# Bisection of a top-k selection: the decision steps move from VectorE to GpSimd

## The chip, the cores and the metric

The kernel runs on one core of a Trainium2 chip. The metric is the device time of one execution in microseconds (us). The engines are TensorE (PE in the profile, PEld for its weight loads), VectorE (DVE), ScalarE (ACT), GpSimd (POOL) and SyncE (SP). Each engine takes its instructions strictly in the order in which they were written into its queue, and engines wait for each other through semaphores.

## The reference

One layer of an encoder on 2048 tokens of width 1024: a combined projection, a sparse attention in which every query keeps its 256 best keys by an index score, a pooling mixer, gates, an output projection with layer norm, and a gated MLP with a short convolution. The part that the change touches is the choice of the keys:

```
rel = relu(einsum('bqhd,bsd->bqhs', qib, k_idx) * idx_scale)
idx_score = einsum('bqh,bqhs->bqs', wib * head_w_scale, rel)
idx_score = where(admissible, idx_score, -inf)
_, sel = top_k(idx_score, topk)        # topk = 256
...
s = where(valid, einsum('bqhd,bqkd->bqhk', qb, k_sel) * attn_scale, -inf)
p = softmax(s)
```

## The kernel before

The 2048 queries are 16 blocks of 128 rows; a row of a block is one partition. The keys of a block are a mask that is computed ahead of the attention, by finding for each row the 256th largest score.

**Bisection.** `select` (L896) finds that threshold bit by bit: 32 rounds from bit 31 down to bit 0. It works on two *halves* of the blocks in turn, so that the decision on one half can run while the other half is counted. For a half and a bit, every block of the half is counted at the trial threshold `F`: ScalarE counts the back part of the scores with a Sign activation that sums (`ca`, L945), VectorE the front part with a comparison that sums (`cd`, L948). Then `decide` (L917) makes the next threshold from the two sums in three steps on VectorE: `g = 2*cd - ca`, `h = (g < lim) * 2^bit`, `F = h xor 2^(bit-1) xor F`. A decision of one half is a generator (`pend`), and one of its steps is taken after each block of the other half's counting (L950), the rest at that half's end (L953). The tiles of a decision have one number per block, so they are 128x2 or 128x4.

**Three selections.** `GROUPS` (L64) gives three selections: blocks 2 and 3 against 4 to 7 (halves of two and four blocks), then 8 and 9 against 10 and 11, then 12 and 13 against 14 and 15. They run as background work: `turn` (L356) gives them a step whenever the projections on TensorE have earned a credit in a cost model, so index scores, counts and decisions are written between the matmuls of `proj_index`, `proj_pool`, `proj_q` and `proj_gates`, and between the instructions on ScalarE and VectorE that empty PSUM for them. `PS1` (L299) has four PSUM banks for these matmuls.

**GpSimd beside it.** In the first of four token groups the projection weights are split into a rounded part and a remainder (`Weights.split` L237, `split` L309): on GpSimd, in pieces of 256 columns (`PIECE`, L95), a TENSOR_SCALAR for the rounded part and a TENSOR_TENSOR for the remainder. A weight item is two tensors of 128x4x256, so eight pieces; its split is written when the item ahead of it is fetched (`get`, L247). Later token groups reload the parts from DRAM. GpSimd also sums the windows of the pooling mixer (L707). So its queue holds much work in the time of the first selection, and little in the others.

Nearly all compute instructions carry the line of the helper that records them (L150); tiles tell them apart. `b` is a tile of the big pool (scores, weights and their parts), `m` one of the pool of eight middle tiles, `p` a PSUM bank.

Of the kernel before, what the change touches and what calls it, by code (L numbers as in the profile page):

```python
# [15 lines left out]
OP = mybir.AluOpType  # L16
# [3 lines left out]
P = 128  # L20
# [236 lines left out]
class Kern:  # L257
# [638 lines left out]
    def select(self, halves):  # L896
# [6 lines left out]
        nc = self.nc  # L903
# [12 lines left out]

        def decide(k, bit):  # L917
            cd, ca = acc[k]
            nh = len(halves[k])
            g_ = self.sml([P, 4], tag="g")[:, :nh]  # L920
            h = self.sml([P, 4], I32, tag="h")[:, :nh]
            f2 = self.sml([P, 4], I32, tag="F")[:, :nh]
            lim = 2.0 * TOPK - 1.0 - ws[k]
            nc.vector.scalar_tensor_tensor(g_, cd, 2.0, ca, op0=OP.mult, op1=OP.subtract)
            yield
            if bit == 31:
                nc.vector.tensor_scalar(h, g_, lim, -1.0, op0=OP.is_lt, op1=OP.mult)
                yield
                nc.vector.tensor_scalar(f2, h, 0x40000000, None, op0=OP.bitwise_xor)
            else:  # L930
                nc.vector.tensor_scalar(h, g_, lim, float(2 ** bit), op0=OP.is_lt, op1=OP.mult)
                yield
                nc.vector.scalar_tensor_tensor(f2, h, 2 ** (bit - 1) if bit else 0, F[k],
                                               op0=OP.bitwise_xor, op1=OP.bitwise_xor)
            F[k] = f2

        pend = None
        for bit in range(31, -1, -1):
            for k, half in enumerate(halves):
                f = F[k].bitcast(F32)  # L940
                w, nh = ws[k], len(half)
                cd, ca = self.sml([P, 4], tag="cd")[:, :nh], self.sml([P, 4], tag="ca")[:, :nh]
                for i, b in enumerate(half):
                    ja, jd = self.M([P, 1024], BF16), self.M([P, 1024], BF16)
                    nc.scalar.activation(ja[:, :w], back[b], AF.Sign, bias=f[:, i:i + 1], scale=-1.0,  # L945
                                         accum_out=ca[:, i:i + 1])
                    n = front[b].shape[1]
                    nc.vector.tensor_scalar(jd[:, :n], front[b], f[:, i:i + 1], None, op0=OP.is_ge, op1=OP.add,  # L948
                                            accum_out=cd[:, i:i + 1])
                    if pend:  # L950
                        next(pend, None)
                    yield
                if pend:  # L953
                    for _ in pend:
                        pass
                acc[k] = (cd, ca)
                pend = decide(k, bit)
        for _ in pend:
            pass
        for k, half in enumerate(halves):  # L960
            f = F[k].bitcast(F32)
            w, nh = ws[k], len(half)
# [19 lines left out]
            for i, b in enumerate(half):  # L982
# [9 lines left out]
                                               op0=OP.mult, op1=OP.subtract)  # L992
# [882 lines left out]
```

## Time and profile before

| | |
|---|---|
| median of 3 runs | 3335.93 us (3323.9, 3339.29, 3335.93) |
| the profiled execution, own time | 3325.95 us |
| its span, first to last instruction | 3324.2 us |
| PE busy | 3168.4 us (95%), 15918 matmuls |
| DVE busy | 2423.5 us (73%) |
| ACT busy | 1585.2 us (48%) |
| POOL busy | 1271.3 us (38%) |
| mean granted clock of TensorE | 0.981 |

The first selection counts from 210 to 416 us of the span, the second from about 530 to 712 us, the third from about 874 to 1083 us. The rest of the 3324 us is attention, output projection and MLP, which the change doesn't touch. How to read it: a share of the whole span says little here, since 95% for PE is a mean over stages; what counts is which engine waits in the three selections.

### The profile page before, as it was taken

Reading aid. Unit: us, or ns where it says so; the run is one execution under the profiler, and the core shown is the slowest. Engines: PE = TensorE matmul, PEld = TensorE weight load, DVE = VectorE, ACT = ScalarE, POOL = GpSimd, SP = SyncE. Lnnn points to the kernel's source line nnn. Section 1 sums busy time; section 2 is a strip of 40 time slices with the busy share of each in tenths; the row PEclk is TensorE's granted clock in tenths of the full one; section 3 lists DMA queues with packets and bytes.
Section 4 is the critical chain, followed back from the end, with each engine's and each line's share of the span. In section 5 each row is a group of like instructions: output and inputs, shape, how many; then the busy total and the mean of one; then the engine's idle time right before and its main releaser. Section 6 shows DMA issues by size and latency. Waiting matters only on the chain. (4 is left out here: it accounts for less than half of the span.)

```text
span 3324.2 us, 46905 instructions
## 1 busy us (share of the span) xinstructions
PE 3168.4 (95%) x15918; PEld 2658.2 (80%) x15918; DVE 2423.5 (73%) x4475; ACT 1585.2 (48%) x2854; POOL 1271.3 (38%) x1302
## 2 busy tenths in 40 slices
PE   8998899999999899999999989999989999999898
PEld 8887688888898778888878877777868778888687
DVE  5589878996899887777676576666578765555597
ACT  3465737855678566666621133333244432223343
POOL 3139400010010787667731154550066511211684
PEclk9999899999999999999999999999999999999999
DMA  8457755754566344443464458997697665666884
GB/s 323 146 197 279 246 210 186 249 198 145 189 249 224 120 162 173 143 158 145 149 231 161 157 209 319 348 328 278 226 356 273 206 250 221 235 248 244 314 308 167
DMA packets 325679, 745.71 MB, mean 224 GB/s; under 512 B 30074, under 2 KB 115006, under 8 KB 325438
## 3 DMA queue, kind: packets, MB, share of 16 engines
q1 hardware_dynamic: 315646, 724.88, 60.8%
q10 hardware_dynamic: 9792, 17.83, 1.4%
q8 instruction: 126, 2.06, 0.3%
q14 instruction: 115, 0.94, 0.1%
HBM read 514.36 MB, written 228.23 MB: 223 GB/s over the span
## 5 line engine op out<-in xcount | busy, mean ns | idle before, releaser
L150 PE MATMUL p<-b,b 128*128 128x512 f32 (+3 forms) x12644 | 2785.6, 369 | 79.5 <-ACT b L150 20.6
L150 PEld LDWEIGHTS p<-b,b 128*128 128x128 f32 x12644 | 2173.6, 191 | 484.0 <-ACT b L150 23.1
L150 ACT ACTIVATE b<-p 128x512 fp32r<-128x512 f32 (+9 forms) x726 | 428.7, 612 | 667.9 <-PE p L150 628.1
L150 ACT ACTIVATE b<-b 128x1024 fp32r<-128x1024 f32 (+2 forms) x248 | 253.2, 1027 | 397.7 <-POOL b L150 148.9
L150 DVE TENSOR_TENSOR b<-b,b 128x1024 fp32r<-128x1024 f32 (+5 forms) x246 | 358.6, 1488 | 78.9 <-ACT b L150 75.9
L150 ACT ACTIVATE m<-b,F 128x448 bf16<-128x448 f32 (+3 forms) x448 | 366.1, 820 | 84.2 <-DVE F L150 67.3
L150 DVE TENSOR_SCALAR_CACHE_REDUCE m<-b,F 128x512 bf16<-128x512 f32 (+6 forms) x476 | 370.8, 808 | 17.8 <-DMA q<-m 12.4
L150 POOL TENSOR_TENSOR b<-b,b 128x256 fp32r<-128x256 f32 (+3 forms) x276 | 315.9, 1161 | 72.3 <-ACT b L150 66.2
L150 DVE TENSOR_TENSOR m<-m,p 128x512 f32<-128x512 f32 x176 | 120.5, 685 | 245.2 <-ACT b L150 207.0
L150 POOL TENSOR_TENSOR b<-b,m 128x512 f32<-128x512 f32 x110 | 196.7, 1808 | 237.9 <-DMA b<-h 165.3
L150 POOL TENSOR_TENSOR m<-b,b 128x512 f32<-128x512 f32 x99 | 144.4, 1466 | 349.4 <-issue 258.4
L150 DVE SCALAR_TENSOR_TENSOR b<-b,cw,b 128x1023 f32<-128x1023 f32 (+1 forms) x176 | 243.4, 1385 | 35.7 <-ACT b L150 34.5
L150 POOL TENSOR_SCALAR b<-b 128x256 fp32r<-128x256 f32 (+3 forms) x216 | 117.3, 558 | 379.4 <-DMA b<-in_w_in_dram 127.7
L150 PE MATMUL p<-b 128*128 128x512 f32 x616 | 235.8, 399 | 13.2 <-ACT b L150 8.7
L150 DVE TENSOR_TENSOR b<-p,b 128x512 fp32r<-128x512 f32 (+1 forms) x286 | 201.5, 713 | 59.5 <-ACT b L150 57.2
L150 PE MATMUL p<-ident,b 128*128 128x128 f32 x1456 | 214.8, 277 | 20.9 <-ACT b L150 14.4
L150 DVE CUSTOM_DVE_ANT_0 b<-p,b 128x1024 f32<-128x1024 f32 (+7 forms) x192 | 173.9, 908 | 67.4 <-PE p L150 66.1
L150 PEld LDWEIGHTS p<-ident,b 128*128 128x128 f32 x1456 | 176.6, 142 | 53.5 <-ACT b L150 17.5
L150 ACT ACTIVATE b<-b,mx 128x1024 f32<-128x1024 f32 (+7 forms) x192 | 171.6, 896 | 67.2 <-DVE mx L150 63.0
L150 DVE SCALAR_TENSOR_TENSOR b<-b,ws,b 128x768 f32<-128x768 f32 (+5 forms) x154 | 157.4, 1050 | 43.1 <-ACT b L150 41.0
L150 ACT ACTIVATE m<-p 128x512 f32<-128x512 f32 (+1 forms) x180 | 105.4, 593 | 152.9 <-PE p L150 136.9
L150 PE MATMUL p<-kst,b 128*128 128x384 f32 (+3 forms) x656 | 151.6, 361 | 4.5 <-DVE b L150 3.3
(126 smaller groups left out, 2386.7 us busy)
## 6 DMA issues: line engine op xcount, KB each, us to landing
b<-uw SPq DMA_DIRECT2D x308, 512.0 KB, 6.8
b<-wp SPq DMA_DIRECT2D x192, 512.0 KB, 6.2
uw<-l SPq DMA_DIRECT2D x98, 512.0 KB, 2.9
b<-in_w_ffn_down_dram SPq DMA_DIRECT2D x154, 256.0 KB, 5.4
b<-h SPq DMA_DIRECT2D x154, 256.0 KB, 5.4
wp<-b SPq DMA_DIRECT2D x64, 512.0 KB, 5.6
uw<-b SPq DMA_DIRECT2D x56, 512.0 KB, 5.4
h<-m SPq DMA_DIRECT2D x110, 256.0 KB, 5.6
```

The source lines that it names most:

```text
L150: return f(*args, **kw)
```

## The change

`decide` keeps its arithmetic and gets one step more. The two sums are now combined on GpSimd in place, in `cd`: `cd = 2*cd - lim`, then `cd = cd - ca`. The comparison `h = (cd < 0) * 2^bit` follows on GpSimd too. Only the xor stays on VectorE. So a decision was three instructions on VectorE and is three on GpSimd and one on VectorE; there are 192 decisions (three selections, 32 bits, two halves).

```diff
         def decide(k, bit):
             cd, ca = acc[k]
+            pool = nc.gpsimd
             nh = len(halves[k])
-            g_ = self.sml([P, 4], tag="g")[:, :nh]
...
             lim = 2.0 * TOPK - 1.0 - ws[k]
-            nc.vector.scalar_tensor_tensor(g_, cd, 2.0, ca, op0=OP.mult, op1=OP.subtract)
+            pool.tensor_scalar(cd, cd, 2.0, -lim, op0=OP.mult, op1=OP.add)
+            yield
+            pool.tensor_tensor(cd, cd, ca, op=OP.subtract)
             yield
             if bit == 31:
-                nc.vector.tensor_scalar(h, g_, lim, -1.0, op0=OP.is_lt, op1=OP.mult)
+                pool.tensor_scalar(h, cd, 0.0, -1.0, op0=OP.is_lt, op1=OP.mult)
                 yield
                 nc.vector.tensor_scalar(f2, h, 0x40000000, None, op0=OP.bitwise_xor)
             else:
-                nc.vector.tensor_scalar(h, g_, lim, float(2 ** bit), op0=OP.is_lt, op1=OP.mult)
+                pool.tensor_scalar(h, cd, 0.0, float(2 ** bit), op0=OP.is_lt, op1=OP.mult)
                 yield
                 nc.vector.scalar_tensor_tensor(f2, h, 2 ** (bit - 1) if bit else 0, F[k],
                                                op0=OP.bitwise_xor, op1=OP.bitwise_xor)
```

Where the new instructions stand shows in the queues of the built programs. First GpSimd, early in the first selection, at the second weight item that is split there (`b_3030`, `b_3040` the rounded parts of its two tensors, `b_3031`, `b_3041` the remainders; `halo` is the pooling mixer's). Before the change:

```order
L150 COPY b_3020<-halo_93 128x16
L150 COPY b_3023<-halo_93 128x16
L150 TENSOR_SCALAR b_3030<-b_2859 128x256 x2
L150 TENSOR_TENSOR b_3031<-b_2859,b_3030 128x256 x2
L150 TENSOR_SCALAR b_3030<-b_2859 128x256 x2
L150 TENSOR_TENSOR b_3031<-b_2859,b_3030 128x256 x2
L150 TENSOR_SCALAR b_3040<-b_2861 128x256 x2
L150 TENSOR_TENSOR b_3041<-b_2861,b_3040 128x256 x2
L150 TENSOR_SCALAR b_3040<-b_2861 128x256 x2
L150 TENSOR_TENSOR b_3041<-b_2861,b_3040 128x256 x2
```

GpSimd at the same place after the change, from the third decision of the selection (`cd_2968`, `h_2990`) to the first instruction of the fourth (`cd_2984`):

```order
L150 TENSOR_SCALAR cd_2968<-cd_2968 128x2
L150 TENSOR_TENSOR cd_2968<-cd_2968,ca_2969 128x2
L150 TENSOR_SCALAR h_2990<-cd_2968 128x2
L150 TENSOR_SCALAR b_3030<-b_2858 128x256 x2
L150 TENSOR_TENSOR b_3031<-b_2858,b_3030 128x256 x2
L150 TENSOR_SCALAR b_3030<-b_2858 128x256 x2
L150 TENSOR_TENSOR b_3031<-b_2858,b_3030 128x256 x2
L150 TENSOR_SCALAR b_3040<-b_2860 128x256 x2
L150 TENSOR_TENSOR b_3041<-b_2860,b_3040 128x256 x2
L150 TENSOR_SCALAR b_3040<-b_2860 128x256 x2
L150 TENSOR_TENSOR b_3041<-b_2860,b_3040 128x256 x2
L150 TENSOR_SCALAR cd_2984<-cd_2984 128x4
```

The split item itself has not moved; two decisions now stand around it, and the fourth has all of its eight pieces ahead of it. The other decisions of the first selection are placed in the same manner, some ahead of an item, some behind it, some between its pieces.

Then VectorE at the same place. Before the change, the end of the second decision and the third (`g_2974` to `F_2976`, `g_2990` to `F_2992`) among the counts (`m,cd<-b,F`):

```order
L150 TENSOR_SCALAR m_2971,cd_2968<-b_1707,F_2751 128x128
L150 SCALAR_TENSOR_TENSOR g_2974<-cd_2743,ca_2744 128x4
L150 TENSOR_SCALAR h_2975<-g_2974 128x4
L150 TENSOR_SCALAR m_2979,cd_2968<-b_1811,F_2751 128x256
L150 TENSOR_SCALAR F_2976<-h_2975 128x4
L150 TENSOR_SCALAR m_2987,cd_2984<-b_2119,F_2976 128x192
L150 SCALAR_TENSOR_TENSOR g_2990<-cd_2968,ca_2969 128x2
L150 TENSOR_SCALAR h_2991<-g_2990 128x2
L150 SCALAR_TENSOR_TENSOR F_2992<-h_2991,F_2751 128x2
```

VectorE after the change, from the same count on:

```order
L150 TENSOR_SCALAR m_2971,cd_2968<-b_1707,F_2750 128x128
L150 TENSOR_SCALAR F_2975<-h_2974 128x4
L150 TENSOR_SCALAR m_2978,cd_2968<-b_1811,F_2750 128x256
L150 TENSOR_SCALAR m_2987,cd_2984<-b_2119,F_2975 128x192
L150 SCALAR_TENSOR_TENSOR F_2991<-h_2990,F_2750 128x2
```

Two of three instructions of a decision are gone; the xor that is left stands where it stood and reads `h` from GpSimd. The places of ScalarE's counts among its other instructions are the same as before in the first selection, within two instructions, and those of TensorE's matmuls among each other nearly so.

## The prediction

> **What bounds the kernel now.** I read the page's slices first, to see where TensorE falls short.
>
> ```profile
> PE   8998899999999899999999989999989999999898
> DVE  5589878996899887777676576666578765555597
> POOL 3139400010010787667731154550066511211684
> PEclk9999899999999999999999999999999999999999
> ```
>
> A slice is 83 us. TensorE is the limit nearly everywhere; one of its dips, and the one dip of the granted clock below 0.9, lies in slices 3 to 5 (166 to 416 us), where VectorE is at 8 to 9 tenths and GpSimd reaches 9. That is the first selection. The windows view puts numbers on the three selections (the first in two parts):
>
> ```profile
> core 0: us, PE busy (x) PEld busy (x) DVE busy (x) ACT busy (x) POOL busy (x), PEclk, DMA share, GB/s
> ...
> 210.00:335.00 125.00, 105.77 (x626) 94.58 (x624) 115.39 (x314) 74.82 (x226) 106.69 (x194) 0.93 0.77 276
> 335.00:415.00 80.00, 66.25 (x273) 53.16 (x274) 71.40 (x285) 65.01 (x199) 38.70 (x73) 0.87 0.73 253
> ...
> 530.00:712.00 182.00, 176.94 (x905) 151.74 (x904) 163.59 (x507) 144.54 (x314) 6.43 (x15) 0.99 0.68 240
> ...
> 874.00:1083.00 209.00, 207.08 (x1110) 179.37 (x1109) 193.50 (x505) 167.92 (x313) 16.65 (x27) 1.00 0.66 235
> ```
>
> From 530 to 712 and from 874 to 1083 us TensorE is busy 97 and 99% at full clock: there it is the bound, and relief of VectorE is worth at most the 5.1 and 1.9 us that it idles. In the first selection it idles 19.2 + 13.8 = 33 us, and VectorE (92% and 89%) and GpSimd (85% in the first part) are full. The waits view of 210 to 415 us names the chain:
>
> ```profile
> ACT m L150 <- DVE F L150: 43.6, 22, 7.4
> ...
> POOL b L150 <- PE p L150: 18.4, 1, 18.4
> PE p L150 <- ACT m L150: 18.3, 5, 5.4
> ...
> PE p L150 <- ACT b L150: 14.0, 7, 4.8
> POOL b L150 <- DMA b<-in_w_in_dram: 11.2, 2, 10.8
> ```
>
> ScalarE waits 43.6 us for the next threshold `F`, and TensorE 32.3 us for ScalarE, which stands behind its counts. So this stage is set by how fast decisions follow each other.
>
> **Why decisions are slow there.** The groups of `g` and `h` in 210 to 335 us, and from the timeline one `g` with what GpSimd did beside it:
>
> ```profile
> L150 DVE SCALAR_TENSOR_TENSOR g<-cd,ca 128x2 f32<-128x2 f32 x15 | 16.5, 1098 | 4.3 <-ACT m L150 4.2
> ...
> L150 DVE SCALAR_TENSOR_TENSOR g<-cd,ca 128x4 f32<-128x4 f32 x16 | 13.3, 828 | 0.9 <-ACT m L150 0.6
> ...
> L150 DVE TENSOR_SCALAR h<-g 128x2 int32<-128x2 f32 x15 | 7.4, 492 | 0.4
> ...
> L150 DVE TENSOR_SCALAR h<-g 128x4 int32<-128x4 f32 x16 | 5.8, 360 | 0.5
> ```
>
> ```profile
> 219.22 8.38 DVE L150 SCALAR_TENSOR_TENSOR g<-cd,ca 128x4 f32<-128x4 f32 x1
> ...
> 219.69 1.44 POOL L150 TENSOR_TENSOR b<-b,b 128x256 fp32r<-128x256 f32 x2
> ...
> 226.08 1.44 POOL L150 TENSOR_TENSOR b<-b,b 128x256 fp32r<-128x256 f32 x2
> ...
> 227.47 0.33 POOL L150 COPY b<-halo 128x16 f32<-128x16 f32 x2
> ```
>
> ```profile
> 318.87 10.97 DVE L150 SCALAR_TENSOR_TENSOR g<-cd,ca 128x2 f32<-128x2 f32 x1 [2.95 <-ACT m L150]
> ...
> 355.27 4.43 DVE L150 SCALAR_TENSOR_TENSOR g<-cd,ca 128x4 f32<-128x4 f32 x1
> ```
>
> A four-number instruction takes 8.38 us while GpSimd runs split pieces back to back, and ends at 227.6, when the pieces end. Three such waits cost 8.38 + 10.97 + 4.43 = 23.8 us; `g` and `h` together hold VectorE for 43.0 of the 125 us. In the quiet selections a `g` takes 172 ns:
>
> ```profile
> L150 DVE SCALAR_TENSOR_TENSOR g<-cd,ca 128x2 f32<-128x2 f32 x128 | 22.1, 172 | 9.0 <-ACT m L150 5.9
> ```
>
> The Trainium skill ("SBUF — State Buffer", section "Who interferes with whom") says that a VectorE instruction with two SBUF inputs contends with a GpSimd instruction that reads SBUF, and that the loser is blocked for that whole instruction. The trace agrees on who is hit, not on how long: by that rule `g` would lose one piece, under 0.8 us, and the three waits, having another cause, would stay, which adds their 24 us to the sum below: 3384 instead of 3360.
>
> **The change: what goes.** `g` and `h` leave VectorE, and the three long waits with them: -24 us on the chain. The xor also has two inputs, but its worst is short, by the view of tile `F` for 205 to 420 us:
>
> ```profile
> L150 DVE SCALAR_TENSOR_TENSOR F<-h,F x62: 148/163/1648, 217.0 to 419.3; 128x2 int32<-128x2 int32 x31, 128x4 int32<-128x4 int32 x31
> ```
>
> 1.65 us; so I carry no long wait over, and price that as a rival.
>
> **What comes: decisions queue behind weight splits.** The price of a piece (210 to 415 us), and of a round on ScalarE, from the timeline's first counts of four rounds:
>
> ```profile
> L150 POOL TENSOR_TENSOR b<-b,b 128x256 fp32r<-128x256 f32 x120 | 87.7, 755 | 0.7 <-POOL b L150 0.7
> L150 POOL TENSOR_SCALAR b<-b 128x256 fp32r<-128x256 f32 x120 | 47.4, 415 | 88.1 <-ACT m L150 49.6 <-PE p L150 18.4 <-DMA b<-in_w_in_dram 11.2
> ```
>
> ```profile
> 366.64 0.67 ACT L150 ACTIVATE m<-b,F 128x448 bf16<-128x448 f32 x1
> ...
> 387.07 0.67 ACT L150 ACTIVATE m<-b,F 128x448 bf16<-128x448 f32 x1 [1.55 <-DVE F L150]
> ...
> 391.00 0.67 ACT L150 ACTIVATE m<-b,F 128x448 bf16<-128x448 f32 x1 [0.23 <-DVE F L150]
> ...
> 413.85 0.67 ACT L150 ACTIVATE m<-b,F 128x448 bf16<-128x448 f32 x1
> ```
>
> A piece is 0.415 + 0.755 = 1.17 us, an item of eight 9.4 us. From the first of these counts to the last are ten rounds (four 128x448 and two 128x256 counts each), with the stage's other work and little waiting: 47.2 / 10 = 4.7 us a round. The round from 387.07 to 391.00 holds nothing but its counts: 3.9 us. GpSimd's own new steps have no row; the nearest are its other tiny ones:
>
> ```profile
> L150 POOL TENSOR_TENSOR m<-head,b 128x2 f32<-128x2 f32 x1 | 0.2, 196 | 4.9 <-DVE m L150 4.9
> ...
> L150 POOL TENSOR_SCALAR lv<-mv 128x1 f32<-128x1 f32 x16 | 16.4, 1022 | 136.5 <-DVE mv L150 136.3
> ```
>
> From 0.2 us undisturbed to 1.0 where a long VectorE instruction runs beside it; I take 0.2 (beside VectorE run mostly counts), so 0.6 a decision and 0.9 with the handovers and the xor (0.16). The other end, three times 1.0, makes a decision 3.3 us; it stays in the range.
>
> Now the cover. A decision is done 0.9 us after its half's counts end; the threshold of the next decision is needed one round, 4.7 us, after that same end. That leaves 3.8 us, of which the next decision takes 0.9: **2.9 us of split work fit between two decisions for nothing, the rest stops ScalarE**, and behind ScalarE's stopped count stand the instructions that empty PSUM for TensorE; behind VectorE's xor, likewise, stand its counts and subtractions. In GpSimd's new queue I added up, from decision to decision, the pieces that stand between (with 1.15 us for a window sum of the pooling mixer). 120 pieces lie between the first and the last decision of the first selection, as many as ran there before. At 12 places they come to 6.3 to 18.7 us, 110 together; at 7 places to 3.1 to 4.7, 28 together; at the rest to less than the cover. Stalls: 110 - 12 x 2.9 + 28 - 7 x 2.9 = **83 us**.
>
> How long the selection took before, from the same view of tile `F`:
>
> ```profile
> L150 ACT ACTIVATE m<-b,F x189: 492/654/671, 210.1 to 415.8; 128x448 bf16<-128x448 f32 x127, 128x256 bf16<-128x256 f32 x62
> ```
>
> That is 206 us for 31.5 rounds (the first half is counted before). After: 31.5 x 4.7 = 148, plus 83, is 231 us: **+25 us**. The three long waits are in the 206 and not in the 231, so they are credited already. Two things are left out and about cancel: the first part has more other work than 4.7 a round holds (ScalarE busy 74.8 us, 15.5 rounds of pure counts of 3.9 make 60), which lies in the stalls' shadow in part; and TensorE's lead of some PSUM banks, each 24 matmuls by the row
>
> ```profile
> L150 PE MATMUL p<-b,b 128*128 128x256 f32 x384 | 53.7, 304 | 8.4 <-ACT b L150 7.8 <-POOL b L150 0.6
> ```
>
> so 24 x 53.7 / 384 = 3.4 us a bank, about 10 us for three.
>
> **Selections two and three: nothing.** GpSimd is busy 6.4 of 182 and 16.7 of 209 us, a half's counts (two blocks) cover a decision of 0.9 us, and TensorE is the bound. If that cover were gone, each of 128 decisions would cost 0.4 us more (0.9 against three steps of 0.17), 51 us at most; that needs VectorE to reach the xor before GpSimd, and it is 90% busy there. SP's queue and the DMAs are the same in number; no DMA moves to GpSimd. A DMA that lands late now stops the decisions behind its split: such waits (11.2 for `w_in`, 18.4 for a buffer held by TensorE) cost nothing before, as GpSimd had no one behind it.
>
> The sum: 3325.95 + 25 = 3351 us against the profiled execution; the median of the three runs is 10 us above that execution, so I say **3360**, and give the times below on that scale too.
>
> **Rivals.** *VectorE's relief decides, faster (0.15).* In the first part 15.5 rounds took 125 us, 8.1 a round, not 4.7. If other work paces them still, the cover there is 8.1 - 1.8 = 6.3 us, and the stalls of that part's twelve places fall from 63 to 30, against 43.0 us of `g` and `h`: -13. The second part's 20 then lie under TensorE's lead, and at best the 33 us in which TensorE idles are won: 3303 to 3323. The turning point is a cover near 5 us. For it speaks VectorE at 92%; against it, that the second part has rounds at 4.7.
> *TensorE doesn't feel it (0.27).* The PSUM lead and ScalarE's free 50 us of 125 swallow most of the 25: 3326 to 3350. Against it: TensorE already waits 32.3 us behind ScalarE.
> *The contention moves on to the xor (0.08, slower).* GpSimd starts its pieces just when it has released the xor, so the xor gets the three long waits: 3360 + 24 = 3384, and 3336 + 83 = 3419 if nothing is won or hidden. The Trainium skill ("Perfetto Trace Analysis", section "Optimizing Scalar/DVE Operations") warns that the two engines share a read port, so that moving operations between them might not help; by that alone the change would win nothing on VectorE.
>
> **How the numbers follow.** The forecast has 0.50, 3350 to 3375, nearly all of it slower. The range runs from 3319 (half the stalls: 148 + 42 against 206 is -16) to 3410, short of the last rival's end; what is left out below is most of the first rival, and I take the lower edge down to 3312 for half of it. A measurement of this kernel can tell about 0.5%, 17 us, from no change: faster 0.15, same 0.27, slower 0.58.
>
> **What would show it.** Right: in 210 to 460 us ScalarE's waits for `F` grow from 43.6 to some 80 us, VectorE's busy time falls by 40 to 60 us, an `h` on GpSimd ends a burst of pieces, TensorE idles 50 us or more there, and everything behind 530 us only shifts. Wrong: TensorE's idle time there falls below 33 us, or the time is lost after the first selection.

## The result, and the profile after

| | before | after |
|---|---|---|
| median of 4 runs each, same chip | 3336.11 us | 3383.64 us |
| the profiled execution, own time | 3325.95 us | 3378.58 us |
| its span | 3324.2 us | 3376.6 us |
| mean granted clock of TensorE | 0.981 | 0.973 |

The change makes the kernel slower: the ratio is 1.0147, with a 95% interval from 1.0119 to 1.0175, which is +47.5 us by the medians. I forecast +24 us (3360 against 3336): the sign and the range (3312 to 3410) held, the size was half.

The page's slices after, to be read against those of before (83 us a slice there, 84 here):

```profile
PE   8986899999999889999999998999999999999998
...
DVE  5555468787788787777766666566669765555697
...
POOL 3147731230032677767652145441048511111584
PEclk9998899999999989999999999999999999999999
```

VectorE has fallen from 8 and 9 to 4 and 5 tenths in the first selection (slices 3 to 5), and TensorE has not gained by it: its dip there is deeper, down to a 6. A second place has come up, in slices 14 and 15 (1097 to 1266 us): the clock is an 8 in the second of them, and TensorE an 8 in both, where before only one was. The windows view (times, then busy time of PE, PEld, DVE, ACT, POOL, then the granted clock, DMA share and GB/s) gives both places:

```profile
210.00:335.00 125.00, 90.16 (x526) 82.06 (x524) 59.20 (x218) 62.38 (x191) 99.85 (x231) 0.84 0.64 226
335.00:460.00 125.00, 109.88 (x445) 87.73 (x446) 64.73 (x266) 78.37 (x238) 83.30 (x226) 0.92 0.65 229
...
1109.00:1160.00 51.00, 39.52 (x190) 32.62 (x188) 36.29 (x90) 17.94 (x43) 35.72 (x41) 0.87 0.28 92
```

TensorE idles 34.8 + 15.1 = 50 us in the first selection, against 33 us before, at a granted clock of 0.84 and 0.92. The waits view of 210 to 460 us shows who waits for whom (total, times, longest):

```profile
DVE F L150 <- POOL h L150: 123.5, 59, 11.9
ACT m L150 <- DVE F L150: 93.3, 27, 12.2
POOL cd L150 <- DVE m L150: 41.0, 30, 3.4
...
PE p L150 <- ACT b L150: 19.4, 6, 5.5
...
PE p L150 <- ACT m L150: 15.2, 3, 8.0
POOL cd L150 <- ACT m L150: 10.7, 9, 2.9
PE p L150 <- POOL b L150: 8.4, 4, 6.4
...
PE p L150 <- DVE m L150: 6.0, 4, 2.3
```

The xor on VectorE waits 123.5 us for `h` from GpSimd, and ScalarE's counts wait 93.3 us for the xor (43.6 us before). TensorE's own waits for ScalarE are 19.4 + 15.2 = 34.6 us, hardly more than the 32.3 us of before. What is new in TensorE's waits is 8.4 us for GpSimd's weight pieces and 6.0 us for VectorE; the same view of the kernel before has for pieces:

```profile
PE p L150 <- POOL b L150: 0.6, 1, 0.6
```

The timeline of GpSimd, VectorE and ScalarE at one decision shows where a decision stands now:

```profile
224.69 0.76 POOL L150 TENSOR_SCALAR b<-b 128x256 fp32r<-128x256 f32 x2
225.43 1.41 POOL L150 TENSOR_TENSOR b<-b,b 128x256 fp32r<-128x256 f32 x2
...
226.82 0.76 POOL L150 TENSOR_SCALAR b<-b 128x256 fp32r<-128x256 f32 x2
...
227.56 1.41 POOL L150 TENSOR_TENSOR b<-b,b 128x256 fp32r<-128x256 f32 x2
...
229.05 0.19 POOL L150 TENSOR_SCALAR cd<-cd 128x4 f32<-128x4 f32 x1
...
230.18 0.23 POOL L150 TENSOR_SCALAR h<-cd 128x4 int32<-128x4 f32 x1
...
230.45 0.16 DVE L150 SCALAR_TENSOR_TENSOR F<-h,F 128x4 int32<-128x4 int32 x1 [7.16 <-POOL h L150]
...
230.70 0.67 ACT L150 ACTIVATE m<-b,F 128x448 bf16<-128x448 f32 x1 [6.70 <-DVE F L150]
```

The split item's last pieces end at 229 us, then the decision runs: VectorE has waited 7.16 us for it, ScalarE 6.70 us. The steps themselves are short (groups in 210 to 460 us: busy, mean ns of one):

```profile
L150 POOL TENSOR_SCALAR h<-cd 128x4 int32<-128x4 f32 x32 | 7.9, 247 | 2.6
...
L150 POOL TENSOR_TENSOR cd<-cd,ca 128x2 f32<-128x2 f32 x31 | 7.0, 225 | 2.4 <-ACT m L150 0.7
...
L150 POOL TENSOR_SCALAR cd<-cd 128x4 f32<-128x4 f32 x32 | 6.6, 206 | 37.0 <-DVE m L150 29.5 <-ACT m L150 6.4
```

That decisions stand behind pieces agrees with the forecast. That TensorE's new waits are not for ScalarE does not, and neither does the second place. Beyond the first selection I had everything "only shift". I followed how late TensorE is in the trace, the n-th matmul against the n-th of the profile of before (negative is earlier; between the 2597th and the 6569th the order differs, so there the row says only how far TensorE has come):

| matmul | starts before at | after is late by |
|---|---|---|
| 1400 | 205.2 us | -1.0 us |
| 2400 | 432.6 us | 27.6 us |
| 3400 | 608.9 us | 35.5 us |
| 5800 | 1065.2 us | 31.6 us |
| 6600 | 1230.2 us | 46.5 us |
| 15800 | 3285.3 us | 52.5 us |

Some 30 us are lost by the end of the first selection, little that stays in the second and third, and then another 15 us between 1065 and 1230 us and 5 us by 1406 us, where no decision runs any more.

### The profile page after: what moved, and what is told of

The parts are those of the page before. It is cut to its first block, busy times and chain, and to the rows that moved or that the text cites. A ratio compares the mean times of both kernels' runs of the same rounds, so it can differ in the third digit from the quotient of the medians.

```text
span 3376.6 us, 47200 instructions
## 1 busy us (share of the span) xinstructions
PE 3188.6 (94%) x15918; PEld 2672.1 (79%) x15918; DVE 2329.7 (69%) x4091; ACT 1584.6 (47%) x2854; POOL 1403.4 (42%) x1878
## 5 line engine op out<-in xcount | busy, mean ns | idle before, releaser
L150 PEld LDWEIGHTS p<-b,b 128*128 128x128 f32 x12644 | 2188.9, 192 | 530.2 <-POOL b L150 37.9
L150 ACT ACTIVATE m<-b,F 128x448 bf16<-128x448 f32 (+3 forms) x448 | 366.1, 819 | 123.5 <-DVE F L150 113.5
L150 PE MATMUL p<-ident,b 128*128 128x128 f32 x1456 | 214.6, 275 | 23.8 <-DVE b L150 13.7
L150 POOL TENSOR_SCALAR cd<-cd 128x2 f32<-128x2 f32 x192 | 40.3, 210 | 449.8 <-DVE m L150 397.1
```

The source lines that it names most:

```text
L150: return f(*args, **kw)
```

## The experiments

**Two causes taken apart.** TensorE's order in the changed kernel differs from that of before from its 2597th matmul on, in the second and third selection too. The planner does that: `turn` gives the background work a step as long as it has credit, and takes off what the step costs on VectorE or ScalarE by the cost model,

```
self.credit -= max(work["dve"] - before["dve"], work["act"] - before["act"])
```

so that decisions that leave VectorE change where later steps are written. I made four kernels that hold the two effects apart: the engine of the steps, and the charge to the planner. Edit of the first (steps on GpSimd, charged as the old ones were on VectorE):

```diff
+            self.charge(0.07 + nh * 0.00104)
             pool.tensor_scalar(cd, cd, 2.0, -lim, op0=OP.mult, op1=OP.add)
             yield
+            self.charge(0.07 + nh * 0.00052)
             pool.tensor_tensor(cd, cd, ca, op=OP.subtract)
...
+            self.charge(0.07 + nh * (0.00052 if bit == 31 else 0.00104))
```

Here `charge` adds its cost to the model's VectorE clock and work, and `pool` and the xor's engine are taken so that the planner doesn't count them itself. TensorE's order is then row for row that of before.

> The three new steps stay on GpSimd in all three selections, but the planner is charged for them as it was for the old steps on VectorE, so TensorE's order is that of the kernel before. Queue theory (decisions wait behind weight splits in the first selection, and nothing else matters): about +47 us as in the changed kernel, with TensorE 35 us late at 560 us and the rest lost behind the third selection. Plan theory (the 16 to 21 us lost behind 1083 us come from the changed order, because decisions that cost VectorE nothing in the cost model change the credit of the background work): +30 to +36 us, near 3369, and nothing lost behind 1083 us.

Measured: 3362.52 us against 3328.86 us of before, ratio 1.0102 [1.0081, 1.0122], +33.7 us, as the plan theory has it (+30 to +36). Its profile still loses 13 us behind 1065 us, where that theory had nothing; more on this below.

The second is the opposite: the three old steps stay on VectorE, `g` and `h` uncharged and the xor charged one step later, as in the changed kernel. TensorE's order is row for row that of the changed kernel.

> The old steps on VectorE, but the planner is charged as in the changed kernel, so TensorE's order is that of the changed kernel. Queue theory: no change from before, 3336 within 5 us. Plan theory: +12 to +21 us, 3348 to 3357, lost behind the third selection (1083 us), nothing in the first.

Measured: 3340.63 us, ratio 1.0035 [1.0022, 1.0048], +11.8 us, at the lower edge of the plan theory. The order alone costs that.

The third and fourth have the order of before and move the steps in some selections only:

```diff
+            if len(halves[1]) == 2:
...
+                F[k] = f2
+                return
+            self.charge(0.07 + nh * 0.00104)
             pool.tensor_scalar(cd, cd, 2.0, -lim, op0=OP.mult, op1=OP.add)
...
```

What is left out first are the three old steps on VectorE. I had this condition the wrong way round: the second half has four blocks in the *first* selection. So the run named e3_first_on_vector has the steps on GpSimd in the first selection only, and e4_first_on_gpsimd (with `== 4`) in the second and third only. The two expectations are to be read crosswise.

> Order of before; the steps run on VectorE in the first selection (as before) and on GpSimd in the second and third. My prediction's term of nothing for these two selections: 3336 within 5 us. Rival, GpSimd's queue at the end of the third selection (splits of the next weights stand behind decisions there): +8 to +21 us, 3344 to 3357.

> Order of before; the steps run on GpSimd in the first selection only. Queue theory: the loss of the first selection alone, +25 (my term) to +36 us (TensorE's lag at 560 us in the changed kernel), 3361 to 3372; ScalarE waits some 90 us for F, against 44 before. Rival, the loss comes from the longer chain of steps, not from the queue: under +10 us.

Measured: GpSimd in the **first** selection only (e3), 3359.07 us, ratio 1.0087 [1.0064, 1.011], +30.2 us. GpSimd in the **second and third** only (e4), 3324.78 us, ratio 0.999 [0.998, 1.0], -4.1 us. The first lies in what the queue theory expected of the first selection (+25 to +36), the second in my term of nothing (within 5 us). The waits of e3 in 205 to 460 us:

```profile
DVE F L963 <- POOL h L961: 112.6, 57, 11.5
ACT m L150 <- DVE F L963: 84.9, 32, 10.5
```

How late TensorE is in these four, against the profile of before (e1, e3 and e4 have exactly its order of matmuls):

| matmul | e1 all GpSimd, old order | e2 VectorE, new order | GpSimd in the first only | in 2 and 3 only |
|---|---|---|---|---|
| 1400 | -3.3 | 2.4 | -2.3 | -1.1 |
| 2400 | 26.2 | 1.6 | 27.7 | 1.3 |
| 5800 | 22.8 | 4.4 | 30.3 | 1.2 |
| 6600 | 23.6 | 14.8 | 30.5 | 1.7 |
| 15800 | 36.2 | 15.2 | 27.3 | 0.5 |

The loss of the first selection goes with GpSimd's steps, most of the loss behind 1065 us with the order. Engine and order together, e1 and e2, are 33.7 + 11.8 = 45.5 us of 47.5. By selection the parts are 30.2 - 4.1 + 11.8 = 37.9 us: e1, with all steps on GpSimd, took 33.7, where 30.2 - 4.1 = 26.1 would be the sum, and its profile loses 8 us between 1230 and 1406 us that no other of the four has. Of these, 5.5 us fall on matmuls 7350 to 7395. The same place loses 3.9 or 5.5 us in the profiles of the changed kernel, of r3, e5, e6b, e7b and c1 below, and nothing in all others. In r3, e5, e6b and e7b no decision of the second and third selection runs on GpSimd, and in r3 and e6b none at all, so the move is not what makes it; what does is open. The 8 to 10 us lie about within the intervals (7 us either way for e1 and e3).

**Where the order costs.** The charge of the changed kernel in the third selection only (from block 12 on), all decisions on VectorE:

> Decisions on VectorE; the planner is charged as in the kernel before in the first and second selection, and as in the changed kernel in the third. If the 12 us that the changed order costs come from the attention's first items, which the order of the third selection pushes behind the mask: +8 to +14 us, with TensorE waiting some 9 us for ScalarE once near 1110 us. If they come from the order in the first two selections: no change, within 4 us of before.

Measured: 3345.44 us against 3330.92, ratio 1.004 [1.0027, 1.0053], +14.5 us. So the order in the third selection alone costs as much as that in all three (+11.8), within the intervals. The timelines of TensorE and GpSimd at the end of that selection (this profile's execution took 3356.84 us; in that of e2, of 3341.55 us, TensorE's wait is the same, 9.79 us):

```profile
1059.73 45.49 PE L150 MATMUL p<-b,b 128*128 128x512 f32 x200
1114.99 0.69 PE L150 MATMUL p<-b,b 128*128 128x128 f32 x2 [9.77 <-ACT b L150]
```

```profile
1089.79 0.77 POOL L150 TENSOR_SCALAR b<-b 128x256 fp32r<-128x256 f32 x2 [27.24 <-ACT b L150]
1090.71 5.10 POOL L150 TENSOR_TENSOR b<-b,b 128x256 fp32r<-128x256 f32 x2
1095.77 2.79 POOL L150 TENSOR_SCALAR b<-b 128x256 fp32r<-128x256 f32 x2
...
1112.45 1.40 POOL L150 TENSOR_TENSOR b<-b,b 128x256 fp32r<-128x256 f32 x2
```

The same of the kernel before:

```profile
1104.46 4.81 PE L150 MATMUL p<-b,b 128*128 128x128 f32 x26 [1.42 <-DVE b L150]
```

```profile
1079.39 0.77 POOL L150 TENSOR_SCALAR b<-b 128x256 fp32r<-128x256 f32 x2 [23.57 <-PE p L150]
1080.13 1.43 POOL L150 TENSOR_TENSOR b<-b,b 128x256 fp32r<-128x256 f32 x2
...
1093.53 2.77 POOL L150 TENSOR_TENSOR b<-b,b 128x256 fp32r<-128x256 f32 x2
```

And of the changed kernel:

```profile
1138.73 0.69 PE L150 MATMUL p<-b,b 128*128 128x128 f32 x2 [8.65 <-ACT b L150]
```

```profile
1113.44 0.78 POOL L150 TENSOR_SCALAR b<-b 128x256 fp32r<-128x256 f32 x2 [6.16 <-ACT b L150]
1114.43 5.10 POOL L150 TENSOR_TENSOR b<-b,b 128x256 fp32r<-128x256 f32 x2 [0.21 <-POOL b L150]
...
1114.96 4.05 DVE L150 TENSOR_TENSOR_SCAN b<-b 128x1664 f16<-128x1664 f16 x1
```

The first piece of the next weight split waits for TensorE before, and for ScalarE with the new order. The waits of that one instruction, as the built programs of before and of r3 have them:

```
before: TENSOR_SCALAR b_13596<-b_13417 128x256 [waits DMAHW5_49,DMAHW6_49,DMAHW0_49,DMAHW7_49,PE_49,Pool_49]
r3:     TENSOR_SCALAR b_13601<-b_13433 128x256 [waits DMAHW5_49,DMAHW6_49,Activation_49,Pool_49]
```

With the new order the mask of the selection takes its buffers ahead of this split, and the piece then waits for ScalarE: it starts right behind ScalarE's first mask instruction (two of them from 1088.70 us, 1.87 us together). The built programs name the buffer: in r3 the split's tile takes that of a score tile (`b_10082`), whose last reader is this mask instruction, before that of a weight tile (`b_13210`), whose last reader is TensorE. So the split can't start before the mask does. It starts 10 us later than before; TensorE was 6.7 us late already at this place of the execution, so some 4 us of the 10 are this wait. Then its pieces run beside VectorE's scan of the mask: a pair of TENSOR_TENSOR pieces takes 5.10 us instead of 1.43, and the twelve pieces up to the last line shown take 24.1 us instead of 16.9. TensorE waits 9.77 us, once. I did not try the new order with another buffer. About 8 us of the order's cost fall here, in r3 and in e2; between matmuls 6376 and 6600 both lose 4.5 to 4.7 us more, which I did not follow.

**Is it the queue, or the length of the chain?** The same pair of kernels with short pieces: the remainders of the projection weights are left out and the rounded part stands in for them, so that a piece is 0.41 us instead of 1.17 (the rest of the edit hands the rounded part on as `lo`).

```diff
...
                 nc.gpsimd.tensor_scalar(hi[:, c], src[:, c], 1.0, 1.0, op0=OP.mult, op1=OP.mult)
-                nc.gpsimd.tensor_tensor(lo[:, c], src[:, c], hi[:, c].bitcast(F32), op=OP.subtract)
+                if lo is not hi:
+                    nc.gpsimd.tensor_tensor(lo[:, c], src[:, c], hi[:, c].bitcast(F32), op=OP.subtract)
```

> The kernel before without the remainders of the projection weights: their TENSOR_TENSOR pieces on GpSimd are left out and the rounded part is used twice, so a piece is 0.415 us instead of 1.17 us. It is the base line of the next run. Fewer long waits of g beside GpSimd: 3300 to 3336 us.

> As the run before it (remainders left out), with the decisions of the first selection on GpSimd, the order as before. Queue theory: by my own sum (pieces between two decisions beyond 2.9 us) the stalls fall from 71 us to 7 us, so the run is within 8 us of its base line, perhaps below it. Rival, the length of the chain of four steps over two engines: it doesn't depend on the pieces, so the loss of 30 us stays.

Measured: 3296.4 us with VectorE, 3302.02 us with GpSimd in the first selection: +5.6 us where the whole pieces gave +30.2. The intervals of the two (0.9873 to 0.9919 and 0.9892 to 0.9947 of before) overlap. The base line came out some 4 us below the range expected of it and 38 us below the kernel before (3334.56), so leaving the remainders out shortens the selection by itself, with VectorE deciding. ScalarE's waits for the threshold, first with VectorE, then with GpSimd:

```profile
ACT m L150 <- DVE F L150: 17.3, 17, 2.2
```

```profile
DVE F L965 <- POOL h L963: 57.4, 56, 4.2
...
ACT m L150 <- DVE F L965: 20.1, 21, 2.1
```

Short pieces, and the same chain over two engines costs ScalarE some 5 us more (20.1 us, and 2.4 us at the first decision, whose xor stands in another line): nearly all of the 57.4 us that VectorE waits for `h` is covered. So the loss comes with the long pieces in the queue, not with the longer chain.

**Or do the pieces wait for the decisions?** A queue works both ways: pieces behind a decision wait for its counts, and weights come late. The kernel before, with three idle steps on GpSimd at the decisions' places in the first selection:

```diff
+            if idle:
+                pool.tensor_scalar(x, cd, 2.0, -lim, op0=OP.mult, op1=OP.add)
             nc.vector.scalar_tensor_tensor(g_, cd, 2.0, ca, op0=OP.mult, op1=OP.subtract)
             yield
+            if idle:
+                pool.tensor_tensor(x, x, ca, op=OP.subtract)
...
+                if idle:
+                    pool.tensor_scalar(y, x, 0.0, float(2 ** bit), op0=OP.is_lt, op1=OP.mult)
```

> The kernel before, with decisions on VectorE; in the first selection GpSimd runs the three new steps as well, at the same places in its queue, into tiles that nobody reads (and the sums have 8 buffers instead of 4, so that VectorE need not wait for their readers). Nothing waits for GpSimd's steps, but the weight pieces behind them wait for the counts. If the loss of the first selection comes from decisions that stand behind pieces: no change, within 5 us of before. If it comes from pieces that stand behind decisions (weights late for TensorE): +15 to +30 us. If VectorE and GpSimd disturb each other over the sums: +5 to +15 us.

Measured: 3327.16 us against 3334.56, ratio 0.998 [0.9967, 0.9993], 7.4 us *faster*. So the steps as such delay no piece by much: TensorE waits 2.4 us for pieces (0.6 before). But the run doesn't settle the question for the changed kernel. Here GpSimd's steps find the counts ready, and wait 0.8 us for VectorE's; in the changed kernel they wait 41.0 us for VectorE's counts and 10.7 us for ScalarE's, as the waits above show, with pieces behind them, and there TensorE waits 8.4 us for pieces (10.2 in e3). Late decisions make late counts, and late counts late pieces: that they follow from each other in this way is argued, and the share of each direction in the 30 us is open.

To see whether the gain comes from the additional buffers for the sums:

> The kernel before with 8 buffers instead of 4 for the two sums; every instruction at its old place. It is the base line for the run with idle steps, which had this edit too. If the 7 us won there come from the buffers: -7 us here. If they come from GpSimd's idle steps, which break its bursts of pieces: no change, within 3 us.

Measured: 3330.1 us against 3330.92, ratio 0.9999 [0.999, 1.0009]: it does not; it comes from the idle steps.

**What the long waits of `g` were worth.** In the run with idle steps they are gone; the view of tile `g` in 205 to 425 us (shortest, median and longest in ns), first before, then with idle steps:

```profile
L150 DVE SCALAR_TENSOR_TENSOR g<-cd,ca x63: 148/163/10966, 212.5 to 417.7; 128x4 f32<-128x4 f32 x32, 128x2 f32<-128x2 f32 x31
```

```profile
L150 DVE SCALAR_TENSOR_TENSOR g<-cd,ca x63: 146/176/1452, 210.4 to 408.3; 128x4 f32<-128x4 f32 x32, 128x2 f32<-128x2 f32 x31
```

10.97 us has become 1.45 us, and the kernel gains 7.4 us of the 23.8. The waits of the run with idle steps in 205 to 425 us show where the rest went:

```profile
PE p L150 <- ACT b L150: 16.5, 6, 4.4
ACT m L150 <- DVE F L150: 14.7, 13, 2.7
...
PE p L150 <- ACT m L150: 5.1, 2, 3.8
...
PE p L150 <- POOL b L150: 2.4, 4, 0.7
```

ScalarE waits 28.9 us less for the threshold (14.7 instead of 43.6), but TensorE only 10.7 us less for ScalarE (21.6 instead of 32.3), and 1.8 us more for pieces. I tried to take the same waits away by the form of the instruction: `g` block by block from one tensor and a scalar operand.

```diff
-            nc.vector.scalar_tensor_tensor(g_, cd, 2.0, ca, op0=OP.mult, op1=OP.subtract)
+            if len(halves[1]) == 4:
+                self.charge(0.07 + nh * 0.00104)
+                for i in range(nh):
+                    self.tc.nc.vector.tensor_scalar(g_[:, i:i + 1], cd[:, i:i + 1], 2.0, ca[:, i:i + 1],
+                                                    op0=OP.mult, op1=OP.subtract)
+            else:
...
```

> All decisions on VectorE in the order of before; in the first selection g is made block by block from one tensor, with the other sum as the scalar operand (2 or 4 instructions instead of 1). If the three long waits of g (23.8 us) come from its second tensor input while GpSimd runs pieces, they vanish and the first selection gets shorter: -5 to -24 us, 3305 to 3324. If any VectorE instruction so small waits there, no change or some us more.

Measured: 3333.15 us against 3334.56, ratio 1.0006 [0.9991, 1.002]: no change. The wait moved to the next instruction; views of tiles `g` and `h`, and the timeline at the longest:

```profile
L932 DVE TENSOR_SCALAR g<-cd,ca x189: 196/207/216, 209.9 to 423.9; 128x1 f32<-128x1 f32 x189
L150 DVE TENSOR_SCALAR h<-g x63: 156/201/17000, 211.4 to 424.2; 128x4 int32<-128x4 f32 x32, 128x2 int32<-128x2 f32 x31
```

```profile
314.14 0.79 POOL L150 TENSOR_SCALAR b<-b 128x256 fp32r<-128x256 f32 x2
314.29 17.00 DVE L150 TENSOR_SCALAR h<-g 128x4 int32<-128x4 f32 x1
...
329.81 1.45 POOL L150 TENSOR_TENSOR b<-b,b 128x256 fp32r<-128x256 f32 x2
```

`h`, one tensor of four numbers, waits 17.00 us through two items and is done when their last piece ends (331.26 us). With the limit of `h` as a scalar operand too (a tile instead of the constant `lim`):

> The run with one-input g again (VectorE, order of before), and h too takes its limit as a scalar operand from a tile instead of as a constant. If the long wait falls on the first small instruction after a count whatever its operands, it moves on to the xor: no change, within 4 us of before. If only instructions without a scalar operand from SBUF wait (all 189 g of the run before took 196 to 216 ns), the long waits go and the first selection gets shorter by a part of their 24 us: -5 to -24 us. The additional instructions cost VectorE some 63 x 2 x 0.2 = 25 us there, which may eat it.

Measured: 3335.36 us against 3333.46, ratio 1.0008 [0.9996, 1.002]. `h` still waits:

```profile
L150 DVE TENSOR_SCALAR h<-g,lim x63: 220/231/12850, 213.2 to 426.6; 128x4 int32<-128x4 f32 x32, 128x2 int32<-128x2 f32 x31
```

Neither reading came out whole: the wait did not move on to the xor, nor does a scalar operand keep an instruction free of it. All the one-number `g` are.

**Versions that might beat both.** Pieces spread instead of written at once (one after each background step, VectorE decides):

```diff
...
             step = next(gen, "end")
+            self.pieces(1)
...
```

Here `pieces(1)` writes the next piece of a list that the split now fills.

> The kernel before, with GpSimd's weight pieces spread: an item's eight pieces are written one after each step of the background work instead of all at once. TensorE's order as before. If VectorE's small instructions wait for the end of GpSimd's bursts, shorter bursts win part of the 24 us of long waits: -3 to -15 us. Rival: pieces written later are late for TensorE: +3 to +15 us, with TensorE waiting for pieces on GpSimd.

Measured: 3325.72 us against 3330.92, ratio 0.9984 [0.9973, 0.9995], 5 us faster. Its profile, of an execution of 3334.51 us, shows no shorter waits: the longest `g` is 10.65 us and the longest `h` 5.35. What gains is open. Idle steps in the first selection and GpSimd's decisions in the other two:

> A candidate, with the order of before: in the first selection decisions on VectorE with the three idle steps on GpSimd between the pieces, in the second and third decisions on GpSimd. If the two small gains (7 us with the idle steps, 4 us with GpSimd in selections two and three) add up: -8 to -12 us, 3323 to 3327; if the second was chance: -5 to -8 us.

Measured: 3321.09 us against 3330.92, ratio 0.9976 [0.9967, 0.9985], 9.8 us faster: the fastest that leaves nothing out. And scalar operands with GpSimd in the other two:

> A candidate: scalar operands for g and h on VectorE in the first selection as in the run before, decisions on GpSimd in the second and third, order of before. If the gain of GpSimd in selections two and three (4 us, beside 10 us for both together with idle steps) is real, 2 to 5 us below the run before it.

Measured: 3329.69 us against 3333.46, ratio 0.9994 [0.9981, 1.0008], 5.7 us below the run with scalar operands alone. So the second and third selection gain 4 to 6 us from the move in two comparisons, the interval of the first reaching up to 1.0; beside the idle steps it is less, the ratio going from 0.998 to 0.9976, with overlapping intervals.

## Why the prediction was half right

- **Decisions queue behind weight splits: right.** Short pieces bring the loss from 30.2 to 5.6 us.
- **"Behind ScalarE's stopped count stand the instructions that empty PSUM": not what grew.** TensorE takes 28.6 us longer for its matmuls 1400 to 2400. Its waits for ScalarE grow by 2.3 us of that (32.3 to 34.6), those for GpSimd's pieces by 7.8 (0.6 to 8.4), those for VectorE by 6.6 (0 to 6.6); and its busy time grows by 11.6 us (194.5 to 206.1) at a granted clock of 0.88 instead of 0.92. My sum had no term for pieces that come late for TensorE.
- **The size of that, +25 us: low by 5, and so near partly by luck.** The first selection alone costs 30.2 us. Stalls were put at 83 us, and ScalarE waits 93.3; the rest of the selection was put at 148 us, and is 247.7 - 93.3 = 154 us, by the counts' view of the changed kernel:

```profile
L150 ACT ACTIVATE m<-b,F x189: 491/652/672, 209.2 to 456.9; 128x448 bf16<-128x448 f32 x127, 128x256 bf16<-128x256 f32 x62
```

  So the selection takes 248 us instead of 231, 42 us more than before and not 25, and TensorE feels some 30 of the 42. I was 17 us too low in the selection's length and let all of it reach TensorE, where some 12 us don't; the two errors nearly cancel.
- **A GpSimd step of 0.2 us, a decision of 0.9: right** (206 to 247 ns; 229.05 to 230.61 us with four copies and a step of the next decision between, 218.15 to 219.17 us without).
- **The long waits go, -24 us: they went, but were worth 7.** Idle steps took nearly all of them away on VectorE, and the time fell by 7.4 us; ScalarE's waits fell by 28.9 us, TensorE's for ScalarE by 10.7.
- **Selections two and three, nothing: right**, even -4.1 us; the cover there holds.
- **"Everything behind 530 us only shifts": this step failed.** I went through the queues of the first selection and left out that the planner, which my own description of the kernel names, is paid by VectorE's cost: it writes the third selection in another order, and that costs 11.8 us by itself (14.5 in the run with that selection alone). My sum had no term for it and the rivals had no such case; the sign that I gave for being wrong, time lost after the first selection, did come. With the measured 12 us, 25 + 12 = 37 us would have been forecast.
- **The rivals.** VectorE's relief did not decide: in 210 to 460 us it is busy 59.20 + 64.73 = 124 us instead of 187 us in 205, and the stage is longer. Contention did not move to the xor: in the changed kernel its longest is 1.0 us. Two of my cases, this one and the one in which the three waits stay, give 3384 us, the measured time to 0.4 us; that is chance, since neither the waits nor a long xor are in the profile.
- **The rule on contention.** The Trainium skill ("SBUF — State Buffer", section "Who interferes with whom") has a second way into that contention, which I had not weighed: a tensor_scalar in a 2-port mode takes the shared pair as well. That the four-number `h` waits, and the 189 one-number `g` don't, is at least no contradiction. A block for one instruction, as that section of the Trainium skill has it, doesn't fit 17.00 us beside 32 piece instructions.

## What to carry to other kernels

Before work that sits on a chain of decisions is put into an in-order queue, look for long bursts in that queue, however idle the engine looks on average (38% here): add up what stands ahead of each step, and compare it with the time until its result is needed; then ask the same of the work that now stands behind the step. Where a planner writes the order from modelled costs, moving an instruction to another engine changes its accounts, and with them the order and the buffers far behind the change: hold the charge fixed to see the engine's effect, and the engine fixed to see the order's. A wait on one engine is worth only what the engines behind it lack of it: here 23.8 us of waits gave 7.

## What the runs showed of the hardware that was not expected

A four-number VectorE instruction beside GpSimd's back-to-back pieces can wait for the whole burst (17.00 us beside 32 piece instructions), on `g` or on `h`, with one tensor input or two, while 189 one-number instructions with a scalar operand took 216 ns at most. Three tiny GpSimd instructions between the bursts, which do no work that is used, took the longest wait from 10.97 to 1.45 us; why they do is not shown. The other way round, GpSimd's pair of TENSOR_TENSOR pieces took 5.10 us instead of 1.43 beside VectorE's scan over 1664 numbers.
